# A decoder layer on one core: in the first feed-forward product, three of eight pairs of weight tiles by seven products, and part of the weight sums added by accumulating transfers

## The chip, the cores and the metric

The kernel runs on one core of a Trainium2 chip. The metric is the device time of one execution in microseconds; the lower the better.

## The reference

One layer of a decoder: a token mixer (an mLSTM group and a dilated attention group), cross-attention into 256 memory tokens, and a SwiGLU feed-forward part, each followed by a residual and a layer norm. All is float32; there are 256 tokens of width 2048. The change lies in the products with `w1` and `w3` (2048 x 5632 each):

```python
def swiglu_ffn(x, w1, w3, w2):
    return (jax.nn.silu(x @ w1) * (x @ w3)) @ w2
...
    y = swiglu_ffn(x, w1[l], w3[l], w2[l])
    x = layer_norm(DEEPNORM_ALPHA * x + y, ln_g[l, 2], ln_b[l, 2])
```

## The kernel before

**Three products for one.** TensorE takes fp32r operands. Each float32 operand is split into a rounded part (`h`, a copy by ScalarE, ACT) and the rest (`l`, a subtraction by VectorE, DVE), both in `split` (L110, L111), and a product is h·h + h·l + l·h: three matmuls of 128x512 for each block.

**The groups.** The first feed-forward product is cut by columns. `f0` is made by `gemm_tokens`; then ten groups `f2`, `f4`, ... `f20` follow, each with 1024 columns (two blocks of 256 of `w1` and of `w3`) by all 2048 rows of weight. The rows are taken as eight *pairs* of tiles, numbered 0 to 7, of two tiles of 128 rows each. Between `f10` and `f12` stand `w2a0` and `w2a1`, the first half of the second feed-forward product; `w2b0` and `w2b1` are the second half. After each group `hidden` takes silu of one half times the other, transposes the result on TensorE (tiles `f8p0`, `f8p1` for group f8), and puts the split transpose into `hT`.

**Plain pairs and pairs by seven products.** A plain pair is 2 tiles x 4 output blocks x 3 = 24 matmuls. For a pair written as a tuple in `plan`, `gemm_seven` uses the scheme with seven products for the eight of a 2x2 by 2x2 block product: 7 x 3 = 21 matmuls. It needs sums of the activations (`mix`, kept for the whole stage as `x2m`) and sums of the weights of the pair. `sums` makes these on DVE in two slots: `t` (two sums, L308, one instruction over 1024 columns) and `s` (two more, L312 and L313, 512 columns each, the second from the first). Of the four tiles that are then split, one is 512 wide and three are 1024 wide. The banks P5, P7 and Q6 belong to the sums; P1, P2, P3, Q4 and E are also or only those of the plain products.

**Buffers.** The weights of a pair (1 MB) come into one of three buffers `w` (`RAW` = 3) by two transfers on SP's queue (SyncE); split tiles go into five `wh`/`wl` buffers (`SPLIT` = 5). Everything else lies in `NSLOT` slots of 128x1024 that `big` takes from the front of a list and `free` puts at its end; `slot` hands out halves of such a slot. A tile that gets a slot waits for the last reader of the tile before it there.

**Order.** A scheduler (in `TileContext`) sets each engine's order at build time from a timeline of its own. On the chip each engine, and each of SP's and GpSimd's (POOL's) queues of transfers, then works strictly in that order, and waits by semaphores.

Of the kernel before, what the change touches and what calls it, by code (L numbers as in the profile page):

```python
# [50 lines left out]
def decoder_layer(ctx: ExitStack, tc: tile.TileContext, A):  # L51
    nc = tc.nc
    V, SC, G, T = nc.vector, nc.scalar, nc.gpsimd, nc.tensor
    CONV = V

    const = ctx.enter_context(tc.tile_pool(name="const", bufs=1))
# [12 lines left out]
    def big(name, dt=F32R):  # L69
        i = free_slots.pop(0)  # L70
        t = up.tile([P, 1024], dt, tag=f"u{i}", name=name)
        held[id(t)] = (i, t)
        return t

    def slot(name):
        if len(free_halves) < 3 and free_slots:
            t = big(name, F32)
            i, _ = held.pop(id(t))
            pair = {"i": i, "free": 2}
            for c in range(2):  # L80
                free_halves.append((t[:, c * 512 : (c + 1) * 512], pair))
        t, pair = free_halves.pop(0)
        pair["free"] -= 1
        held[id(t)] = (pair, t)
        return t

    def free(*tiles):
        for t in tiles:
            where, _ = held.pop(id(t))
            if isinstance(where, int):  # L90
                free_slots.append(where)
                continue
# [27 lines left out]
    class Operand:  # L120
# [79 lines left out]
    def fetch_pair(src, name):  # L200


        def get(b):
            w = wp.tile([P, 2, W], F32, tag="w", name=f"{name}w{b}", bufs=RAW)
            for c in range(2):
                nc.sync.dma_start(
                    out=w[:, :, c * 512 : (c + 1) * 512],
                    in_=src[c][b // 2][:, b % 2].rearrange("p (s c) -> p s c", s=2),
                )
            return w  # L210

        return get

    def plain(get, b, name, kept=()):

# [80 lines left out]
                    op.free(order[n] // 2)  # L296
        return banks

    def sums(get, b, name):

        w = get(b)
        t, t2 = big(f"{name}t{b}", F32), big(f"{name}s{b}", F32)
        q = w.rearrange("p i (c n) -> p (i c) n", c=2)

        V.tensor_tensor(  # L308
            out=t.rearrange("p (c n) -> p c n", c=2), in0=q[:, 0::3], in1=q[:, 1:2].to_broadcast([P, 2, 512]),
            op=ALU.add,  # L310
        )
        V.tensor_tensor(out=t2[:, :512], in0=t[:, :512], in1=q[:, 3], op=ALU.add)  # L312
        V.tensor_tensor(out=t2[:, 512:], in0=t2[:, :512], in1=q[:, 2], op=ALU.add)  # L313
        for to, x, n in (("P1", w[:, 0], 1), (("P2", "P3"), w[:, 1], 2), (("P5", "P7"), t, 2), (("Q6", "Q4"), t2, 2)):
            wh = wp.tile([P, W], F32R, tag="wh", name=f"{name}h{b}")
            wl = wp.tile([P, W], F32R, tag="wl", name=f"{name}l{b}")
            cs = slice(0, 512 * n)
            split(wh[:, cs], wl[:, cs], x[:, cs])
            for i, k in enumerate((to,) if n == 1 else to):
                yield k, wh, wl, slice(i * 512, (i + 1) * 512)  # L320
        free(t, t2)

    def gemm_seven(op, get, nkt, name, plan, early, order=None, kept=range(0), last=False):

        order = order or list(range(nkt))
        of = {i: bank(f"{name}{i}") for i in ("P2", "P3", "Q4", "E", "P1")}  # L330
        of |= {i: sbank(f"{name}{i}") for i in ("P5", "P7", "Q6")}
        banks = [[of["P2"], of["P3"]], [of["Q4"], of["E"]]]
        begun = set()
        final = [b for b in plan if isinstance(b, int)][-1]
        final7 = [b for b in plan if not isinstance(b, int)][-1][0]

        def product(to, lhsT, rhs, end):
            T.matmul(of[to], lhsT, rhs, start=to not in begun, stop=end)  # L338
            begun.add(to)

        def tile_products(m, n, wh, wl, cols=range(2)):
            xh, xl = (op.get(order[n], x, m * P, P) for x in (0, 1))
            for c in cols:
                cs, to = slice(c * 512, (c + 1) * 512), (("P2", "P3"), ("Q4", "E"))[m][c]
                product(to, xh, wh[:, cs], False)
                product(to, xh, wl[:, cs], False)
            for c in cols:
                cs, to = slice(c * 512, (c + 1) * 512), (("P2", "P3"), ("Q4", "E"))[m][c]
                product(to, xl, wh[:, cs], n == 2 * final + 1)

        behind = []
        for step in plan:
            if isinstance(step, int):
                for n, wh, wl in plain(get, step, name, kept):
                    tile_products(0, n, wh, wl)
                    if n in kept:
                        behind.append((n, wh, wl))
                    else:
                        tile_products(1, n, wh, wl)
                b = step  # L360
            else:
                (b,) = step
                j = order[2 * b] // 2
                for to, wh, wl, cs in sums(get, b, name):
                    xh, xl = (op.of_product(to, j, x) for x in (0, 1))
                    product(to, xh, wh[:, cs], False)
                    product(to, xh, wl[:, cs], False)
                    product(to, xl, wh[:, cs], b == final7 and to in ("P1", "P5", "P7", "Q6"))
                if b == final7:
                    early(of)  # L370
            if last and 2 * b not in kept:
                op.free(order[2 * b] // 2)
        for c in range(2):
            for n, wh, wl in behind:
# [38 lines left out]
    def turned(rows, j, name):  # L413
# [15 lines left out]
        out=tri, in_=tri, pattern=[[1, P]], compare_op=ALU.is_ge, fill=NEG, base=0, channel_multiplier=-1  # L429
# [246 lines left out]
    def into_rows(rows, name):  # L676


        def early(of):
            u = slot(f"{name}u")  # L680
            for m in range(2):
                rows.append([slot(f"{name}{m}{c}") for c in range(2)])
            (r11, r12), (r21, r22) = rows
            SC.copy(r11, of["P1"])
            V.tensor_tensor(out=u, in0=r11, in1=of["Q6"], op=ALU.subtract)
            V.tensor_tensor(out=r21, in0=u, in1=of["P7"], op=ALU.add)
            V.tensor_tensor(out=r12, in0=of["P5"], in1=u, op=ALU.subtract)
# [78 lines left out]
    sel_t = slot("sel")  # L766
# [3 lines left out]
    nc.sync.dma_start(out=cw, in_=A["conv"])  # L770
    gb = const.tile([8, 1], F32, tag="gb", name="gb")
    nc.sync.dma_start(out=gb, in_=A["gate_b"])
    gw = const.tile([P, KT, 8], F32, tag="gw", name="gw")
    nc.sync.dma_start(out=gw, in_=A["w_gate"])

    gw2 = const.tile([P, KT, 40], F32R, tag="gw2", name="gw2")
    gz = slot("gwz")
    V.memset(gz, 0.0)
    V.tensor_copy(gw2[:, :, 8:32], gz.rearrange("p (k c) -> p k c", k=KT)[:, :, :24])
# [6 lines left out]
        attention(2 * j, qk0[j], qk0[2 + j], [va[m][0] for m in range(2)], tb)  # L786
    qk1 = in_features(2) + in_features(3)
    es, least_norm = gates()
    free(sel_t)
    for j in range(2):  # L790
        attention(4 + 2 * j, qk1[j], qk1[2 + j], [va[m][1] for m in range(2)], tb)
    free(*va[0], *va[1])
# [14 lines left out]
    for c in range(2):  # L807
        t = slot(f"mg{c}")
# [34 lines left out]
    order = list(range(8, 16)) + list(range(8))  # L843
# [3 lines left out]
    for g in range(2):  # L847
        get, plan = fetch(A["w_out"][g], f"wo{g}"), [0, 2, (1,), 4, 5, (3,), 6, 7]
# [88 lines left out]
    plan = [0, 2, (1,), 4, (3,), 5, 6, 7]  # L937
# [5 lines left out]
    x2 = Operand("x2")  # L943
# [47 lines left out]
            for m in range(2):  # L991
                add(m, c, banks, scale=1.0)

    for j in (2, 5):
        x2.mix_again(j)
    for g in range(2, n, 2):
        get, rows = fetch_pair(A["w13"][g - 2 : g], f"f{g}"), []
        plan = [0, 1, (2,), 3, 4, (5,), 6, 7]
        banks = gemm_seven(x2, get, KT, f"f{g}", plan, into_rows(rows, f"f{g}r"), last=g == n - 2)
        whole(rows, banks)  # L1000
        hidden(g, rows, lambda b, i: [b[i][:, x * 256 : (x + 1) * 256] for x in range(2)], f"f{g}")
        free(*rows[0], *rows[1])
        if g == half - 2:
            w2_first()
# [115 lines left out]
```

## Time and profile before

| | |
|---|---|
| runs | 1546.26, 1546.54, 1547.52 us; median 1546.54 |
| the profiled execution | 1546.63 us, of which the span of the instructions is 1544.8 us |
| TensorE | 1526.1 us busy, 99% of the span |
| VectorE, ScalarE, GpSimd | 77%, 50%, 2% of the span |
| transfers | 301.35 MB, mean 195 GB/s |

In the profile, PE is TensorE's matmuls, PEld its loads of the stationary operand, DVE VectorE, ACT ScalarE, POOL GpSimd, and SPq the transfers that SP issues. A row of instructions has its start, its duration, the engine, the line of the kernel, and what it writes and reads; in brackets stands the time for which the engine was idle before it, and what ended that. Matmuls overlap, so the duration of one is longer than the distance from one to the next.

### The profile page before, as it was taken

Reading aid. Unit: us, or ns where it says so; the run is one execution under the profiler, and the core shown is the slowest. Engines: PE = TensorE matmul, PEld = TensorE weight load, DVE = VectorE, ACT = ScalarE, POOL = GpSimd, SP = SyncE. Lnnn points to the kernel's source line nnn. Section 1 sums busy time; section 2 is a strip of 40 time slices with the busy share of each in tenths; the row PEclk is TensorE's granted clock in tenths of the full one; section 3 lists DMA queues with packets and bytes.
Section 4 is the critical chain, followed back from the end, with each engine's and each line's share of the span. In section 5 each row is a group of like instructions: output and inputs, shape, how many; then the busy total and the mean of one; then the engine's idle time right before and its main releaser. Section 6 shows DMA issues by size and latency. Waiting matters only on the chain.

```text
span 1544.8 us, 19283 instructions
## 1 busy us (share of the span) xinstructions
PE 1526.1 (99%) x7410; PEld 1277.2 (83%) x7410; DVE 1192.9 (77%) x1584; ACT 775.7 (50%) x1011; POOL 30.9 (2%) x30
## 2 busy tenths in 40 slices
PE   9999999999999999999999999999999999999997
PEld 7888888888888888888887888887788888888885
DVE  7665888787789655557788678887788878888897
ACT  5445555554544544444544554555445455555551
POOL 0000000000000000000014000000000000000000
PEclk9999999999999999999999999999999999999999
DMA  8674445674664546445553565665465656668552
GB/s 302 215 266 162 151 171 207 221 256 144 228 214 168 212 169 215 167 139 193 187 191 136 171 210 191 217 193 192 162 218 192 206 191 193 199 193 268 197 189 108
DMA packets 83354, 301.35 MB, mean 195 GB/s; under 512 B 7181, under 2 KB 9402, under 8 KB 59710
## 3 DMA queue, kind: packets, MB, share of 16 engines
q1 hardware_dynamic: 83262, 300.12, 56.3%
q8 instruction: 58, 0.95, 0.2%
q14 instruction: 34, 0.28, 0.1%
HBM read 297.97 MB, written 4.21 MB: 196 GB/s over the span
## 4 chain that ended last, share of the span: by engine, by line
PE 95%; DVE 3%; DMA 1%; issue 1%; ACT 0%; SPq 0%; DVEq 0%; ACTq 0%
PE w2a1P L338 2%; PE w2a0P L338 2%; PE w2b0P L338 2%; PE w2b1P L338 2%; PE f10P L338 2%; PE f20P L338 2%; PE v1P L338 2%; PE xo0P L338 2%; PE xo1P L338 2%; PE v0P L338 1%; PE f18P L338 1%; PE f8P L338 1%; PE wo0P L338 1%; PE f4P L338 1%; PE f2P L338 1%; PE f6P L338 1%
## 5 line engine op out<-in xcount | busy, mean ns | idle before, releaser
L257 DVE TENSOR_TENSOR xv1l<-xv1w,xv1h 128x1024 fp32r<-128x1024 f32 x16 | 19.6, 1224 | 20.7 <-ACT xv1h L256 20.6
L257 DVE TENSOR_TENSOR xv0l<-xv0w,xv0h 128x1024 fp32r<-128x1024 f32 x16 | 19.6, 1225 | 20.0 <-ACT xv0h L256 20.0
L110 ACT CAST w2a1h<-w2a1w 128x1024 fp32r<-128x1024 f32 (+1 forms) x24 | 22.5, 980 | 23.3 <-PE w2a1E L338 14.5
L110 ACT CAST w2a0h<-w2a0w 128x1024 fp32r<-128x1024 f32 (+1 forms) x24 | 22.8, 980 | 17.8 <-PE w2a0E L338 10.7
L111 DVE TENSOR_TENSOR w2a0l<-w2a0w,w2a0h 128x1024 fp32r<-128x1024 f32 (+1 forms) x24 | 26.5, 1131 | 6.1 <-ACT w2a0h L110 6.1
L111 DVE TENSOR_TENSOR w2a1l<-w2a1w,w2a1h 128x1024 fp32r<-128x1024 f32 (+1 forms) x24 | 26.4, 1131 | 5.6 <-ACT w2a1h L110 5.6
L256 ACT CAST xv1h<-xv1w 128x1024 fp32r<-128x1024 f32 x16 | 16.9, 1055 | 23.8 <-PE xv1b L276 17.2
L256 ACT CAST xv0h<-xv0w 128x1024 fp32r<-128x1024 f32 x16 | 16.9, 1055 | 21.6 <-PE xv0b L276 16.4
L110 ACT CAST w2b0h<-w2b0w 128x1024 fp32r<-128x1024 f32 (+1 forms) x20 | 19.2, 988 | 16.8 <-PE w2b0E L338 10.1
L338 PE MATMUL w2a0P<-w2a0h,hT 128*128 128x512 f32 x80 | 26.2, 391 | 0.2 <-ACT w2a0h L110 0.2
L257 POOL TENSOR_TENSOR f0l<-f0w,f0h 128x512 fp32r<-128x512 f32 x12 | 20.0, 1696 | 314.6 <-ACT f0h L256 314.6
L110 ACT CAST w2b1h<-w2b1w 128x512 fp32r<-128x512 f32 (+1 forms) x28 | 19.8, 758 | 12.5 <-PE w2b0E L338 5.4
L338 PE MATMUL w2a1P<-w2a1h,hT 128*128 128x512 f32 x80 | 25.4, 389 | 0.0
L110 ACT CAST wo1h<-wo1w 128x1024 fp32r<-128x1024 f32 (+1 forms) x16 | 15.6, 1000 | 18.9 <-PE wo1E L338 11.3
L110 ACT CAST f12h<-f12w 128x1024 fp32r<-128x1024 f32 (+1 forms) x16 | 15.6, 1000 | 18.7 <-PE f12E L338 11.3
L273 PE MATMUL f0b<-f0l,x 128*128 128x512 f32 x64 | 24.9, 405 | 0.1
L273 PE MATMUL xv0b<-xv0l,mT 128*128 128x512 f32 x64 | 25.0, 391 | 0.0
L111 DVE TENSOR_TENSOR w2b0l<-w2b0w,w2b0h 128x1024 fp32r<-128x1024 f32 (+1 forms) x20 | 22.2, 1139 | 3.6 <-ACT w2b0h L110 3.6
L272 PE MATMUL xv1b<-xv1h,mT 128*128 128x512 f32 x64 | 24.9, 392 | 0.0
L272 PE MATMUL xv0b<-xv0h,mT 128*128 128x512 f32 x64 | 24.9, 389 | 0.0
L273 PE MATMUL xv1b<-xv1l,mT 128*128 128x512 f32 x64 | 24.9, 389 | 0.0
L272 PE MATMUL f0b<-f0h,x 128*128 128x512 f32 x64 | 24.7, 407 | 0.0
(1641 smaller groups left out, 5488.4 us busy)
## 6 DMA issues: line engine op xcount, KB each, us to landing
w2a0w<-in_w SPq DMA_DIRECT2D x12, 1024.0 KB, 4.9
w2a1w<-in_w SPq DMA_DIRECT2D x12, 1024.0 KB, 5.2
w2b0w<-in_w SPq DMA_DIRECT2D x10, 1024.0 KB, 4.9
w2b1w<-in_w SPq DMA_DIRECT2D x10, 1024.0 KB, 5.0
v0w<-in_w_v SPq DMA_DIRECT2D x8, 1024.0 KB, 5.2
v1w<-in_w_v SPq DMA_DIRECT2D x8, 1024.0 KB, 4.9
v2w<-in_w_v SPq DMA_DIRECT2D x8, 1024.0 KB, 4.9
wo0w<-in_w_out SPq DMA_DIRECT2D x8, 1024.0 KB, 6.0
```

The source lines that it names most:

```text
L110: SC.copy(hi, src)
L111: V.tensor_tensor(out=lo, in0=src, in1=as_f32(hi), op=ALU.subtract)
L256: SC.copy(wh[:, cs], w[:, i, cs])
L257: eng.tensor_tensor(out=wl[:, cs], in0=w[:, i, cs], in1=as_f32(wh[:, cs]), op=ALU.subtract)
L272: T.matmul(banks[m][c], xh, wh[:, cs], start=n == 0, stop=False)
L273: T.matmul(banks[m][c], xh, wl[:, cs], start=False, stop=False)
L338: T.matmul(of[to], lhsT, rhs, start=to not in begun, stop=end)
```

## The change

The plan of each of the ten groups goes from two to three pairs by seven products, and these stand as the second, fourth and sixth of the eight steps; before they were the third and the sixth. Correspondingly three activation sums `x2m` are made instead of two. Of the weight sums, `t` is no longer added by DVE: two transfers on SP's queue write one block of weights each into the halves of `t` (0.26 MB each), and a transfer on POOL's queue then reads a third block, once for each half, and adds it to what lies there (`accum_op`, 0.52 MB written). `s` is still made by DVE. There are 35 slots in place of 34; to pay for one, the gate weights `gw` and `gw2` move from places of their own into slots that are freed again.

```diff
-NSLOT, RAW, SPLIT = 34, 3, 5
+NSLOT, RAW, SPLIT = 35, 3, 5
...
-        return get
+        def part(b, s, c):
+            return src[c][b // 2][:, b % 2].rearrange("p (s c) -> p s c", s=2)[:, s : s + 1]
+
+        def get_sums(b, t):
+            t = t.rearrange("p (c n) -> p c n", c=2)
+            nc.sync.dma_start(out=t[:, 0:1], in_=part(b, 0, 0))
+            nc.sync.dma_start(out=t[:, 1:2], in_=part(b, 1, 1))
+            G.dma_start(out=t, in_=part(b, 0, 1).to_broadcast([P, 2, 512]), accum_op=ALU.add)
+
+        return get, get_sums
...
-    def sums(get, b, name):
+    def sums(get, b, name, get_sums=None):
+        t = big(f"{name}t{b}", F32)
+        if get_sums:
+            get_sums(b, t)
         w = get(b)
-        t, t2 = big(f"{name}t{b}", F32), big(f"{name}s{b}", F32)
+        t2 = big(f"{name}s{b}", F32)
         q = w.rearrange("p i (c n) -> p (i c) n", c=2)
-        V.tensor_tensor(
-            out=t.rearrange("p (c n) -> p c n", c=2), in0=q[:, 0::3], in1=q[:, 1:2].to_broadcast([P, 2, 512]),
-            op=ALU.add,
-        )
+        if not get_sums:
+            V.tensor_tensor(
+                out=t.rearrange("p (c n) -> p c n", c=2), in0=q[:, 0::3],
+                in1=q[:, 1:2].to_broadcast([P, 2, 512]), op=ALU.add,
+            )
...
-    gw = const.tile([P, KT, 8], F32, tag="gw", name="gw")
+    gw_t, gw2_t = slot("gw"), big("gw2")
+    gw = gw_t[:, :128].rearrange("p (k c) -> p k c", k=KT)
...
-    gw2 = const.tile([P, KT, 40], F32R, tag="gw2", name="gw2")
+    gw2 = gw2_t[:, :640].rearrange("p (k c) -> p k c", k=KT)
...
-    free(sel_t)
+    free(sel_t, gw_t, gw2_t)
...
-    for j in (2, 5):
+    for j in (1, 4, 6):
         x2.mix_again(j)
     for g in range(2, n, 2):
-        get, rows = fetch_pair(A["w13"][g - 2 : g], f"f{g}"), []
-        plan = [0, 1, (2,), 3, 4, (5,), 6, 7]
-        banks = gemm_seven(x2, get, KT, f"f{g}", plan, into_rows(rows, f"f{g}r"), last=g == n - 2)
+        rows, plan = [], [0, (1,), 2, (4,), 3, (6,), 5, 7]
+        get, get_sums = fetch_pair(A["w13"][g - 2 : g], f"f{g}")
+        banks = gemm_seven(
+            x2, get, KT, f"f{g}", plan, into_rows(rows, f"f{g}r"), last=g == n - 2, get_sums=get_sums
+        )
```

In most groups the scheduler lets the transfers of a `t` run a whole group ahead; those of `f4t4` stand ahead of the first weights of f2. In f10 it does not. The next rows are VectorE's in f10 before, around the sum `f10s2` of its first pair by seven products: `hT8`, `hT9` and `hTm8` are the results of f8 that are put away, `f10l2` are splits of pair 2, `f10l6` is one of the plain pair 3.

```order
L111 TENSOR_TENSOR hT9_8833<-f8p1_8828,hT9_8833 128x2x256 [waits Activation_49]
L144 TENSOR_TENSOR f8ru_8720<-f8r11_8723,f8ru_8720 128x128 [waits DVE_49]
L111 TENSOR_TENSOR f10l2_8940<-f10t2_8917,f10h2_8939 128x1024 [waits Activation_49]
L111 TENSOR_TENSOR hT8_8814<-f8r11_8723,hT8_8814 128x2x256 [waits Activation_49]
L111 TENSOR_TENSOR hTm8_8821<-f8ru_8720,hTm8_8821 128x512 [waits Activation_49]
L312 TENSOR_TENSOR f10s2_8918<-f10t2_8917,f10w2_8914 128x512 [waits DVE_49]
L313 TENSOR_TENSOR f10s2_8918<-f10s2_8918,f10w2_8914 128x512 [waits DVE_49]
L111 TENSOR_TENSOR f10l2_8950<-f10s2_8918,f10h2_8949 128x1024 [waits Activation_49]
L111 TENSOR_TENSOR f10l6_8963<-f10w3_8959,f10h6_8962 128x1024 [waits DMAHW5_49,DMAHW4_49,Activation_49]
```

The same place now, where the first pair by seven products is pair 1 and the second is pair 4; `f10l4_8998` and `f10l5_9014` are the splits of the plain pair 2 that stands between them.

```order
L111 TENSOR_TENSOR hT9_8901<-f8p1_8896,hT9_8901 128x2x256 [waits Activation_49]
L144 TENSOR_TENSOR f8ru_8788<-f8r11_8791,f8ru_8788 128x128 [waits DVE_49]
L111 TENSOR_TENSOR hT8_8882<-f8r11_8791,hT8_8882 128x2x256 [waits Activation_49]
L326 TENSOR_TENSOR f10s1_8954<-f10t1_8947,f10w1_8951 128x512 [waits DVE_49]
L111 TENSOR_TENSOR hTm8_8889<-f8ru_8788,hTm8_8889 128x512 [waits Activation_49]
L327 TENSOR_TENSOR f10s1_8954<-f10s1_8954,f10w1_8951 128x512 [waits DVE_49]
L111 TENSOR_TENSOR f10l1_8985<-f10s1_8954,f10h1_8984 128x1024 [waits Activation_49]
L326 TENSOR_TENSOR f10s4_9036<-f10t4_9029,f10w4_9033 128x512 [waits DMAHW7_49,DMAHW2_49,DMASW6_49]
L111 TENSOR_TENSOR f10l4_8998<-f10w2_8994,f10h4_8997 128x1024 [waits DMAHW5_49,DMAHW4_49,Activation_49]
L111 TENSOR_TENSOR f10l5_9014<-f10w2_8994,f10h5_9013 128x1024 [waits Activation_49]
```

The sum `s` still stands behind `hT8`; the row that adds `f10t4`, which waits for an accumulating transfer (DMASW), now stands ahead of the plain splits. Following `big` and `free` through the code, `f10s1` gets the slot in which `hidden` of f8 had kept the copy that `hT8` is made from, as `f10s2` did before; and `f10t4` gets the slot of `f8h10` and `f8h11`, whose last readers are the transposes into `f8p1`.

TensorE at this place before: the last transposes of f8 and what follows. After them 13 plain matmuls of pairs 0 and 1 follow (three are shown) before the first of pair 2.

```order
L967 MATMUL f8p0_8807<-ident_75,f8r11_8723 128x128 [waits DVE_49]
L967 MATMUL f8p0_8807<-ident_75,f8r01_8722 128x128
L967 MATMUL f8p0_8807<-ident_75,f8r11_8723 128x128
L967 MATMUL f8p1_8828<-ident_75,f8t0_8812 128x128 [waits DVE_49]
L967 MATMUL f8p1_8828<-ident_75,f8t0_8812 128x128 x2
L338 MATMUL f10E_8839<-f10h1_8863,x20_6997 128x512
L338 MATMUL f10Q4_8838<-f10h2_8882,x21_7000 128x512
L338 MATMUL f10Q4_8838<-f10l2_8883,x21_7000 128x512
```

TensorE now: the first `Q6` row reads the ScalarE copy `f10h1_8984` of the sum `f10s1`.

```order
L982 MATMUL f8p0_8875<-ident_75,f8r11_8791 128x128 [waits DVE_49]
L982 MATMUL f8p0_8875<-ident_75,f8r01_8790 128x128
L982 MATMUL f8p0_8875<-ident_75,f8r11_8791 128x128
L982 MATMUL f8p1_8896<-ident_75,f8t0_8880 128x128 [waits DVE_49]
L982 MATMUL f8p1_8896<-ident_75,f8t0_8880 128x128 x2
L352 MATMUL f10P7_8910<-f10h1_8974,x2m1_7404 128x512 [waits Activation_49]
L352 MATMUL f10P7_8910<-f10l1_8975,x2m1_7404 128x512
L352 MATMUL f10P7_8910<-f10h1_8974,x2m1_7404 128x512
L352 MATMUL f10Q6_8911<-f10h1_8984,x2m1_7404 128x512 [waits Activation_49]
L352 MATMUL f10Q4_8906<-f10h1_8984,x21_6995 128x512
L352 MATMUL f10P2_8904<-f10h4_8997,x22_7003 128x512 [waits Activation_49]
L352 MATMUL f10P3_8905<-f10h4_8997,x22_7003 128x512
```

Counted in the program's order, 35 matmuls of f10 stood ahead of this batch of transposes and 63 ahead of the first that reads the copy of the sum `s`; now it is 36 and 39. The fiftieth matmul is the last ahead of the first that reads `f10l4_8998`.

SP's queue in f10 now; the weights `f10w3` stand behind the two plain transfers of `f10t4`. On POOL's queue the accumulating transfers stand in the order `f10t1`, `f10t6`, `f10t4`.

```order
L206 DMA f10w4_9033<-in_w13 128x2x512 [waits DMAHW7_49,DMAHW6_49,DVE_49]
L206 DMA f10w4_9033<-in_w13 128x2x512
L218 DMA f10t6_9111<-in_w13 128x512 [waits DMAHW0_49,DVE_49]
L219 DMA f10t6_9111<-in_w13 128x512 [waits DMAHW1_49]
L218 DMA f10t4_9029<-in_w13 128x512 [waits DMASW3_49,DMAHW2_49,DVE_49,PE_49]
L219 DMA f10t4_9029<-in_w13 128x512 [waits DMAHW3_49]
L206 DMA f10w3_9076<-in_w13 128x2x512 [waits DMAHW4_49,DVE_49]
```

Before, nothing but the sixteen transfers of `f10w` and those of the next stage stood on this queue. In the whole program TensorE's order has 30 matmuls fewer; its order also changes here and there in the token mixer, where the slots are handed out differently.

More of the change, by code (lines that the diff above doesn't have):

```diff
@@ L321, in sums, with gemm_seven @@
         free(t, t2)
-    def gemm_seven(op, get, nkt, name, plan, early, order=None, kept=range(0), last=False):
+    def gemm_seven(op, get, nkt, name, plan, early, order=None, kept=range(0), last=False, get_sums=None):
         order = order or list(range(nkt))
@@ L363, in gemm_seven @@
                 j = order[2 * b] // 2
-                for to, wh, wl, cs in sums(get, b, name):
+                for to, wh, wl, cs in sums(get, b, name, get_sums):
                     xh, xl = (op.of_product(to, j, x) for x in (0, 1))
```

## Prediction

> **What bounds the kernel now.** I read the profile's page first: the span, the busy shares, and the shares of the chain that ended last.
>
> ```profile
> span 1544.8 us, 19283 instructions
> PE 1526.1 (99%) x7410; PEld 1277.2 (83%) x7410; DVE 1192.9 (77%) x1584; ACT 775.7 (50%) x1011; POOL 30.9 (2%) x30
> PE 95%; DVE 3%; DMA 1%; issue 1%; ACT 0%; SPq 0%; DVEq 0%; ACTq 0%
> q1 hardware_dynamic: 83262, 300.12, 56.3%
> ```
>
> TensorE sets the time, and a matmul saved counts in full where it does not begin to wait. The transfers took 56% of the sixteen engines' time, all of them on the hardware queue: no accumulating transfer is in this trace. Then I cut the stage: a plain group (f4), f10, and f16, a group in which a fetch came late. The columns are the stretch, its length, the busy time of each engine with its instructions, granted clock, share and rate of transfers.
>
> ```profile
> core 0: us, PE busy (x) PEld busy (x) DVE busy (x) ACT busy (x) POOL busy (x), PEclk, DMA share, GB/s
> 911.66:954.76 43.10, 43.10 (x195) 35.66 (x195) 36.15 (x47) 23.33 (x29) 0.00 (x0) 1.00 0.61 196
> 1040.99:1085.26 44.27, 43.70 (x196) 35.53 (x195) 34.96 (x45) 23.53 (x29) 0.00 (x0) 1.00 0.57 190
> 1298.50:1342.26 43.76, 43.52 (x195) 35.41 (x194) 36.51 (x47) 23.65 (x29) 0.00 (x0) 1.00 0.60 192
> ```
>
> In a plain group TensorE never stops: 43.10 of 43.10 us, clock 1.00. f10 already loses 44.27 − 43.10 = 1.17 us and f16 loses 0.66 us. The chain of waits gives the step of a matmul and, in f10, the transposes and the place where ScalarE takes over the chain.
>
> ```profile
> 911.66 5.44 PE f4P L338 x24
> ...
> 1040.99 5.44 PE f10P L338 x24
> ...
> 1049.18 0.65 PE f8p L967 x6
> ...
> 1056.43 1.05 ACT f10h L110
> 1057.53 0.73 PE f10P L338 x2
> ```
>
> A matmul takes 5.44 / 24 = 0.2267 us and a transpose 0.65 / 6 = 0.108 us. A group has 6 x 24 + 2 x 21 = 186 matmuls and 8 transposes: 42.17 + 0.87 = 43.04 us, which is the 43.10 read.
>
> **What is removed.** Three matmuls in each of ten groups: 30 x 0.2267 = −6.80 us, all on the path if the cover holds; a group then takes 42.4 us.
>
> **What is added on VectorE and ScalarE.** The next rows are f4's groups of instructions, with mean ns of one behind the bar.
>
> ```profile
> L111 DVE TENSOR_TENSOR f4l<-f4w,f4h 128x1024 fp32r<-128x1024 f32 x11 | 13.3, 1220 | 4.4 <-ACT f4h L110 4.4
> L110 ACT CAST f4h<-f4w 128x1024 fp32r<-128x1024 f32 x10 | 10.1, 1054 | 5.8 <-PE f4E L338 5.8
> L313 DVE TENSOR_TENSOR f4s<-f4s,f4w 128x512 f32<-128x512 f32 x2 | 1.4, 684 | 0.0
> L111 DVE TENSOR_TENSOR f4l<-f4w,f4h 128x512 fp32r<-128x512 f32 x2 | 1.4, 684 | 0.0
> L110 ACT CAST f4h<-f4w 128x512 fp32r<-128x512 f32 x2 | 1.2, 612 | 0.7 <-ACT f4h L110 0.7
> L308 DVE TENSOR_TENSOR f4t<-f4w 128x1024 f32<-128x1024 f32 x1 | 1.2, 1217 | 0.0
> ```
>
> A pair that turns from plain to seven has three splits of 1024 and one of 512 in place of two of 1024, and two sums of 512: on VectorE 1.22 + 0.68 + 2 x 0.68 = +3.3 us, on ScalarE 1.05 + 0.61 = +1.7. Two L308 go, −2.4. VectorE is then busy 36.15 + 0.9 = 37.0 of 42.4 us (87%), ScalarE 25. TensorE's matmuls hide both; without that cover it would be at most 0.9 us a group, since VectorE's total stays below TensorE's. The third `x2m` costs a copy, four blocks and a split on VectorE:
>
> ```profile
> L152 DVE TENSOR_TENSOR x2r<-x 128x512 f32<-128x512 f32 x1 | 0.7, 692 | 0.0
> L141 DVE TENSOR_TENSOR x2r<-x2r 128x128 f32<-128x128 f32 x1 | 0.3, 285 | 0.0
> 850.72 6.67 DVE L257 TENSOR_TENSOR f0l<-f0w,f0h 128x1024 fp32r<-128x1024 f32 x5 [4.60 <-ACT f0h L256]
> ```
>
> 0.69 + 4 x 0.28 + 0.69 = 2.5 us, once. During f0 VectorE has an idle gap of 4.60 us; I take 0, and 2.5 if the gap is gone. The slots for `gw`, `gw2` and the moved order in the token mixer: no row prices them; the nearest is f10's own loss of 1.17, so 0 ± 1.
>
> **f10, the largest term.** Slots are scarcest here, because `hT` has grown. The rows are VectorE's, ScalarE's and TensorE's around the sum `f10s2` of before, in order of time.
>
> ```profile
> 1049.55 0.59 ACT L972 COPY f8r<-f8p 128x512 f32<-128x512 f32 x1 [0.49 <-PE f8p L967]
> 1051.64 1.22 DVE L111 TENSOR_TENSOR f10l<-f10t,f10h 128x1024 fp32r<-128x1024 f32 x1
> 1052.78 0.69 DVE L111 TENSOR_TENSOR hT<-f8r,hT 128x512 fp32r<-128x512 f32 x1
> 1053.38 0.68 DVE L111 TENSOR_TENSOR hTm<-f8ru,hTm 128x512 fp32r<-128x512 f32 x1
> 1053.98 0.68 DVE L312 TENSOR_TENSOR f10s<-f10t,f10w 128x512 f32<-128x512 f32 x1
> 1054.70 0.69 DVE L313 TENSOR_TENSOR f10s<-f10s,f10w 128x512 f32<-128x512 f32 x1
> 1055.48 1.05 ACT L110 CAST f10h<-f10s 128x1024 fp32r<-128x1024 f32 x1 [2.88 <-DVE f10s L313]
> 1056.58 0.50 PE L338 MATMUL f10Q<-f10h,x2m 128*128 128x512 f32 x1 [0.36 <-ACT f10h L110]
> ```
>
> `f10s` takes the slot of f8's copy, so its chain is: transposes, copy, `hT8`, first add, second add, ScalarE's copy, TensorE. Count from f10's first matmul (1040.99). Before, the batch of transposes stood behind 35 matmuls (8.19) and 63 matmuls stood ahead of the sum's reader, so the chain was nearly hidden. Now the batch stands behind 36: 36 x 0.2267 + 2 x 0.108 = 8.38. ScalarE's copy starts 0.37 later, 8.75. From copy to first add it was 1053.98 − 1049.55 = 4.43; the split of `f10t` is no longer in between (−1.14, row to row), and `hTm` now stands behind (−0.60): 11.44. Then `hTm` and the second add at 12.64, ScalarE at +0.78, 13.42 to 14.47, TensorE at 14.5. But TensorE arrives after 39 matmuls and 8 transposes, 8.84 + 0.87 = 9.7: it waits 4.8 us, and about 0.5 more for ScalarE's copy of pair 2's first tile, which comes next. So 5.3 in place of 1.17: **+4.1** from the order alone.
>
> The accumulating transfer follows. VectorE's add that needs `f10t4` now stands ahead of the splits of plain pair 2, and TensorE comes to the first matmul that reads these at 14.5 + 0.5 + 11 x 0.2267 = 17.5. `f10t4` gets the slot that the transposes of f8 free at 8.38 + 0.65 = 9.03; SP then issues two transfers of 0.26 MB (0.42 each, below), the second of which lands after 2.7: 12.2. Then the accumulating one takes X, the add and the split 1.9 more: TensorE goes on at 14.1 + X. What X is, no row shows. The nearest:
>
> ```profile
> f4w<-in_w SPq DMA_DIRECT2D x16, 512.0 KB, 5.1
> xv0w<-in_xv SPq DMA_DIRECT2D x8, 1024.0 KB, 4.9
> z<-in_x SPq DMA_DIRECT2D x6, 256.0 KB, 2.7
> L206 SPq DMA_DIRECT2D f16w<-in_w x16: 367/420/472, 1279.4 to 1320.3; - x16
> L720 POOL TENSOR_TENSOR l1r<-l1r,mhalf 128x1 f32<-128x1 f32 x2 | 2.0, 987 | 3.6 <-DVE l1r L719 3.6
> DVE f16t L308 <- DMA f16w<-in_w: 4.5, 2, 4.0
> ```
>
> (KB, and us from issue to landing; SP's issue min/median/max in ns; in the last row total, times, longest of a wait.) From below X is 2.7: then nothing is added. From above it is two landings one after the other and an instruction of POOL, 2 x 5.1 + 1.0 = 11.2: TensorE stops 7.8 more. It reads and writes 0.52 MB besides fetching 0.52, so I take the row of the same traffic, 5.1, and POOL's 1.0: X = 6.1, TensorE goes on at 20.2 and not 17.5, **+2.8**. f10 thus costs 6.9 more than before.
>
> The Trainium skill, page "DMA: Bandwidth & Descriptors", section "Anatomy of one DMA — SWDGE (gpsimd) path", fits a transfer issued by GpSimd as 2.0 us and its bytes at 436 GB/s; no run here shows one. Taking the bytes twice, 2.0 + 2 x 0.524 / 0.436 gives an estimate for X of 4.4 us, a stop of 1.0, and by that a sum 1.8 us lower than mine, no case of its own. The 1024 KB row above, 4.9 us where the fit has 4.4, leans to my value.
>
> SP's queue: behind `f10t4` stand the weights of pair 3, about 10 us late but needed only after pair 4, 90 matmuls in (20.4 us and the stops). POOL has 30 instructions in all and holds nobody else.
>
> **Contention in the other nine groups.** f4's transfers took 0.61 x 43.10 = 26.3 us of the engines, for 196 GB/s x 43.10 = 8.45 MB: 3.1 us per MB. Added are 3 x 0.52 = 1.57 MB of plain transfers, +4.9 us, and as much accumulated at one or two times the price: 36 to 41 of 42.4 us. It fits, more tightly. A late fetch is in the trace: in f16 VectorE waited 4.0 us for it, and TensorE lost 0.66. Between no group and all nine (5.9) I take two more: **+1.3**.
>
> **Sum:** −6.80 + 6.9 + 1.3 = +1.4. The profiled execution took 1546.63 us, 1.83 more than its span and 0.09 above the median of the runs; 1546.6 + 1.4 = **1548.0**.
>
> **The rivals.**
>
> *The gain arrives.* f10's chain is shorter than I add it up and no fetch comes late. For it: the other nine groups had no stop to speak of and VectorE stays at 87%. Against: even X = 2.7 leaves +4.1 in f10, and that follows from the order. From −6.8 to −6.8 + 3.6: 1539.8 to 1543.4.
>
> *Accumulating transfers slow the weights (ends slower).* The plain and accumulating transfers share the sixteen engines with the weights; an add that waits at a pair's start stands ahead of splits that TensorE needs. It decides from where a weight fetch lands over 4 us late, f16's case, in most groups: nine at 0.66 to 2 us are 6 to 18 on −6.8 + 6.9: 1553 to 1565. Above a price of (42.4 − 31.2) / 4.9 = 2.3 times a plain transfer the engines would bound the group; at 4 times it would be 31.2 + 19.6 = 50.8 us, ten times 7.7 more, over 1620. For it: the share goes from 0.6 to 0.85 or more. Against: the rows show no stage near that limit.
>
> *`f10t4` is late alone.* X = 11.2: 1.3 − 6.8 + 4.1 + 7.8 = +6.4, or 1553.
>
> **How the numbers follow.** Forecast 0.50: f10 at +4.1 to +9, up to three late fetches, 0 ± 1 early, own range 1544 to 1550. The gain arrives 0.20; contention 0.24; `f10t4` late 0.06. A measurement of this kernel tells about 0.2%, 3.1 us, from no change: below 1543.4 is faster, above 1549.6 slower. The forecast gives 0.43 of the 0.50 to the same and 0.07 to slower; faster 0.20, same 0.43, slower 0.07 + 0.24 + 0.06 = 0.37. The range 1542 to 1557 leaves out half of the first rival and about a third of the second with its tail.
>
> **What would show it.** Right: nine groups of about 42.4 us in the chain of waits; in f10 a first `Q` matmul that waits some 4 to 5 us for ScalarE's `f10h`, and a second stop where VectorE waits for `f10t`'s accumulating transfer; f10 at 49 to 51 us; a transfer share of 0.8 or more in the groups. Wrong: f10 under 46 us (the gain arrives), VectorE's adds waiting for `w` or `t` in most groups with TensorE idle at their pairs (contention), or changes in the token mixer above 2 us.

## The result and the profile after

The changed kernel takes 1606.53 us (median; 1602.97 to 1608.96), the kernel before 1546.6 in the same comparison: a ratio of 1.0382, 95% interval 1.037 to 1.0395. It is 60 us slower; the range ended at 1557.

The page of the changed kernel, the same lines as before, and the new queue of GpSimd's transfers:

```profile
span 1606.8 us, 19488 instructions
PE 1542.5 (96%) x7380; PEld 1282.9 (80%) x7380; DVE 1207.7 (75%) x1610; ACT 790.7 (49%) x1032; POOL 65.4 (4%) x60
PE 83%; DMA 8%; DVE 6%; issue 1%; ACT 1%; SPq 0%; DVEq 0%; ACTq 0%
q1 hardware_dynamic: 91902, 315.85, 56.6%
q0 software_dynamic: 8160, 15.73, 5.6%
```

TensorE has the 30 matmuls fewer, yet is busy 16.4 us longer, so the matmuls themselves became slower; and it is idle 64.3 us instead of 18.7 (span less busy time). Transfers hold 8% of the chain instead of 1%. From the first matmul of a stage to the first of the next (us):

| stage | before | changed | difference |
|---|---|---|---|
| start to v2 (token mixer) | 247.6 | 260.3 | +12.7 |
| v2 to f0 | 571.8 | 570.7 | −1.1 |
| f0 | 49.0 | 54.2 | +5.2 |
| f2 | 43.1 | 53.4 | +10.3 |
| f4, f6 | 86.2 | 86.7 | +0.5 |
| f8 | 43.1 | 45.8 | +2.7 |
| f10 | 44.3 | 57.9 | +13.6 |
| w2a0, w2a1, f12 | 170.0 | 170.5 | +0.5 |
| f14 | 43.1 | 49.7 | +6.6 |
| f16, f18 | 87.0 | 85.0 | −2.0 |
| f20 | 43.3 | 56.1 | +12.8 |

So the loss lies at a few places; f6, f16 and f18 take 42.4 to 42.8 us, close to the 42.4 forecast. The stretches f2, f6, f8, f10, f14, f18 and f20 of the changed kernel:

```profile
core 0: us, PE busy (x) PEld busy (x) DVE busy (x) ACT busy (x) POOL busy (x), PEclk, DMA share, GB/s
885.40:938.76 53.36, 47.60 (x192) 37.87 (x192) 37.36 (x44) 27.40 (x33) 2.38 (x2) 0.90 0.76 230
982.66:1025.40 42.74, 42.74 (x192) 34.92 (x192) 36.38 (x48) 25.18 (x31) 2.39 (x2) 1.00 0.76 236
1025.40:1071.31 45.91, 43.71 (x193) 34.92 (x192) 37.46 (x49) 25.38 (x32) 2.38 (x2) 1.00 0.78 231
1071.31:1129.22 57.91, 47.18 (x193) 37.59 (x192) 37.36 (x48) 25.52 (x31) 2.38 (x2) 0.88 0.68 205
1299.75:1349.47 49.72, 45.53 (x193) 37.02 (x192) 36.58 (x48) 25.19 (x31) 3.58 (x3) 0.93 0.82 239
1391.96:1434.40 42.44, 42.44 (x193) 34.99 (x192) 35.53 (x46) 24.62 (x31) 2.38 (x2) 1.00 0.79 248
1434.40:1490.61 56.21, 45.88 (x193) 36.82 (x192) 37.36 (x45) 24.45 (x30) 1.20 (x1) 0.91 0.71 228
```

f6 and f18 have 42.7 and 42.4 us of matmuls and no idle time, with the transfers at 0.76 to 0.79. The four bad groups lose in two columns: idle time (f10: 57.91 − 47.18 = 10.7) and, at a granted clock of 0.88 to 0.93, slower matmuls (f10: 47.18 − 42.4 = 4.8). Over f2, f10, f14 and f20 that is 31 us idle and 16.6 us of slower clock.

What TensorE waited for (its timeline; idle time in brackets), in f2 three times, in f10 twice, in f14 and in f20:

```profile
888.70 0.50 PE L352 MATMUL f2P<-f2h,x 128*128 128x512 f32 x1 [1.58 <-ACT f2h L110]
890.67 0.80 PE L352 MATMUL f2P<-f2h,x 128*128 128x512 f32 x1 [1.47 <-ACT f0h L976]
914.87 0.50 PE L352 MATMUL f2Q<-f2l,x2m 128*128 128x512 f32 x1 [2.63 <-DVE f2l L111]
1085.90 0.79 PE L352 MATMUL f10Q<-f10h,x2m 128*128 128x512 f32 x1 [4.18 <-ACT f10h L110]
1097.07 1.22 PE L352 MATMUL f10P<-f10l,x 128*128 128x512 f32 x2 [6.20 <-DVE f10l L111]
1323.55 0.80 PE L352 MATMUL f14P<-f14l,x2m 128*128 128x512 f32 x1 [4.19 <-DVE f14l L111]
1464.01 0.80 PE L352 MATMUL f20P<-f20l,x2m 128*128 128x512 f32 x1 [9.25 <-DVE f20l L111]
```

And the transfers that the chain of waits names behind these stops:

```profile
871.91 15.60 DMA f2w<-in_w
...
902.35 10.54 DMA f2w<-in_w
...
1085.03 10.13 DMA f10t<-in_w
...
1309.94 10.90 DMA f14w<-in_w
...
1451.28 10.77 DMA f20t<-in_w
```

In f2 and f14 it is a fetch of weights that took 10.5 to 15.6 us (a median of 5.1 and 5.2 before), in f10 and f20 an accumulating transfer that took 10 to 11. In f10 the add for pair 4 waits 8.08 us for the transfer, as forecast, with the splits of pair 2 behind it. In f20 the rows of VectorE show the same blocking: the add for pair 6 waits 11.50 us, and the split of pair 4, which TensorE wants next, stands behind it.

```profile
1095.18 0.69 DVE L326 TENSOR_TENSOR f10s<-f10t,f10w 128x512 f32<-128x512 f32 x1 [8.08 <-DMA f10t<-in_w]
1095.79 2.35 DVE L111 TENSOR_TENSOR f10l<-f10w,f10h 128x1024 fp32r<-128x1024 f32 x2
...
1462.13 0.69 DVE L326 TENSOR_TENSOR f20s<-f20t,f20w 128x512 f32<-128x512 f32 x1 [11.50 <-DMA f20t<-in_w]
1462.74 1.22 DVE L111 TENSOR_TENSOR f20l<-f20t,f20h 128x1024 fp32r<-128x1024 f32 x1
```

How the weights of f2 came to take 15 us: the queues and issues in the 22 us from 868 to 890, around the first matmul of f2 at 885.4 (packets, MB, share of sixteen engines; KB, us to landing).

```profile
q1 hardware_dynamic: 2249, 4.30, 57.2%
q0 software_dynamic: 1073, 2.07, 51.4%
f2w<-in_w SPq DMA_DIRECT2D x8, 512.0 KB, 15.5
f2t<-in_w POOLq DMA_DIRECT2D x2, 512.0 KB, 10.5
```

The shares add up to over 100%: by this measure the engines are full. GpSimd's queue holds 51% of them for 2.07 MB, SP's 57% for 4.30.

### The profile page after: what moved, and what is told of

It is laid out like the page before. It is cut to its first block, busy times and chain, and to the rows that moved or that the text cites. A ratio compares the mean times of both kernels' runs of the same rounds, so it can differ in the third digit from the quotient of the medians.

```text
span 1606.8 us, 19488 instructions
## 1 busy us (share of the span) xinstructions
PE 1542.5 (96%) x7380; PEld 1282.9 (80%) x7380; DVE 1207.7 (75%) x1610; ACT 790.7 (49%) x1032; POOL 65.4 (4%) x60
## 3 DMA queue, kind: packets, MB, share of 16 engines
q0 software_dynamic: 8160, 15.73, 5.6%
## 4 chain that ended last, share of the span: by engine, by line
PE 83%; DMA 8%; DVE 6%; issue 1%; ACT 1%; SPq 0%; DVEq 0%; ACTq 0%
PE w2a0P L352 2%; PE w2b0P L352 2%; PE w2b1P L352 2%; DMA f2w<-in_w 2%; PE f16P L352 1%; PE f10P L352 1%; PE xo0P L352 1%; PE wo0P L352 1%; PE v1P L352 1%; PE v0P L352 1%; PE xo1P L352 1%; PE wo1P L352 1%; PE v2P L352 1%; PE f12P L352 1%; DMA w2a1w<-in_w 1%
## 5 line engine op out<-in xcount | busy, mean ns | idle before, releaser
L267 DVE TENSOR_TENSOR xv1l<-xv1w,xv1h 128x1024 fp32r<-128x1024 f32 x16 | 19.6, 1225 | 20.7 <-ACT xv1h L266 20.6
L110 ACT CAST w2a1h<-w2a1w 128x1024 fp32r<-128x1024 f32 (+1 forms) x24 | 22.6, 980 | 22.5 <-PE w2a1E L352 12.9
L110 ACT CAST w2a0h<-w2a0w 128x1024 fp32r<-128x1024 f32 (+1 forms) x24 | 22.8, 981 | 17.8 <-PE w2a0E L352 10.7
L266 ACT CAST xv1h<-xv1w 128x1024 fp32r<-128x1024 f32 x16 | 16.9, 1055 | 23.8 <-PE xv1b L286 17.2
L266 ACT CAST xv0h<-xv0w 128x1024 fp32r<-128x1024 f32 x16 | 16.9, 1053 | 21.6 <-PE xv0b L286 16.4
L111 DVE TENSOR_TENSOR f2l<-f2w,f2h 128x1024 fp32r<-128x1024 f32 (+1 forms) x16 | 17.4, 1121 | 12.5 <-ACT f2h L110 12.5
L110 ACT CAST f20h<-f20w 128x1024 fp32r<-128x1024 f32 (+1 forms) x16 | 14.9, 968 | 22.1 <-PE f20P L352 10.5
L110 ACT CAST wo1h<-wo1w 128x1024 fp32r<-128x1024 f32 (+1 forms) x16 | 15.6, 1000 | 18.9 <-PE wo1E L352 11.3
```

The lines of the kernel that those rows point to most:

```text
L110: SC.copy(hi, src)
L111: V.tensor_tensor(out=lo, in0=src, in1=as_f32(hi), op=ALU.subtract)
L266: SC.copy(wh[:, cs], w[:, i, cs])
L267: eng.tensor_tensor(out=wl[:, cs], in0=w[:, i, cs], in1=as_f32(wh[:, cs]), op=ALU.subtract)
```

## The experiments

All are timed against the kernel before, in the same comparison 1546.7 to 1547.9 us.

**e1, the slots alone.** In the kernel before:

```diff
-NSLOT, RAW, SPLIT = 34, 3, 5
+NSLOT, RAW, SPLIT = 35, 3, 5
...
-    gw = const.tile([P, KT, 8], F32, tag="gw", name="gw")
-    gw2 = const.tile([P, KT, 40], F32R, tag="gw2", name="gw2")
+    gw_t, gw2_t = slot("gw"), big("gw2")
...
```

> The kernel before with 35 slots in place of 34 and the gate weights in slots; plan of two pairs by seven products and sums by VectorE as before. Theory (the 12.7 us lost in the token mixer come from the slots alone): the first matmul of v2 comes at 260 us and not at 247.6, the feed-forward groups take 43.1 us each, and the time is about 1559 us. Rival (the token mixer's loss hangs on the new plan of the feed-forward part, through the scheduler): v2 at 247.6, about 1546.6 us.

1559.55 us, ratio 1.0082 (1.0067 to 1.0097); v2 begins at 261.9. The token mixer's loss comes from the slots. f0 takes 52.7 here too, so most of f0's loss is theirs as well; f10 gains 1.2 us and w2a0 1.7. Two stretches of e1's mixer around its second stop:

```profile
190.00:200.00 10.00, 7.67 (x44) 6.31 (x42) 3.90 (x12) 2.20 (x7) 0.00 (x0) 1.00 0.08 28
200.00:210.00 10.00, 7.77 (x30) 6.48 (x31) 6.86 (x18) 4.63 (x12) 0.00 (x0) 0.66 0.00 0
```

TensorE is idle for 2.3 and 2.2 us of these stretches, has a mean clock of 0.66 in the second, and almost nothing is transferred; before, it was busy in every one of these 20 us.

**e2, all sums by VectorE.** In the changed kernel:

```diff
-            x2, get, KT, f"f{g}", plan, into_rows(rows, f"f{g}r"), last=g == n - 2, get_sums=get_sums
+            x2, get, KT, f"f{g}", plan, into_rows(rows, f"f{g}r"), last=g == n - 2
```

> The changed kernel with all sums added by VectorE: three pairs by seven products, 35 slots, no transfer for the sums. Theory A (what costs in the feed-forward part is the accumulating transfers): f2, f14 and f20 take 42.4 to 43 us, f10 keeps a first stop of 4 to 5 us for the sum s and what the clock loses after it (47 to 50 us); the token mixer keeps its 12.7; in all 1546.6 + 12.7 - 6.8 + 4 to 8 = 1556 to 1561 us. Rival B (the scarce slots and the order of three pairs by seven products cost it, whoever adds): f2, f14, f20 keep 7 to 13 us each, about 1590 us or more.

1564.79 us, ratio 1.011 (1.0094 to 1.0127), 3.8 above the top of what was expected: the changed kernel loses 41.7 us to something that goes with the transfers. f2, f4, f6, f8, f16, f18 and f20 take 42.4 to 42.5, f14 43.7. f10 takes 51.4, 9.0 over 42.4, without any such transfer: the stop for the sum `s`, and a clock that drops. Its stop, then the whole of f10 and stretches of 1 to 4 us around the stop:

```profile
1071.63 0.79 PE L352 MATMUL f10Q<-f10h,x2m 128*128 128x512 f32 x1 [5.19 <-ACT f10h L110]
```

```profile
1055.92:1107.30 51.38, 45.84 (x193) 36.87 (x192) 39.66 (x50) 25.63 (x31) 0.00 (x0) 0.93 0.52 176
1068.00:1069.00 1.00, 0.00 (x0) 0.00 (x0) 0.93 (x3) 0.45 (x1) 0.00 (x0) 1.00 0.00 0
1070.00:1071.00 1.00, 0.00 (x0) 0.00 (x0) 1.00 (x2) 0.47 (x1) 0.00 (x0) 0.88 0.00 0
1072.00:1073.00 1.00, 1.00 (x3) 0.55 (x3) 1.00 (x2) 1.00 (x2) 0.00 (x0) 0.50 0.97 305
1076.00:1078.00 2.00, 2.00 (x7) 1.53 (x7) 1.93 (x2) 1.01 (x1) 0.00 (x0) 0.60 0.72 240
1078.00:1082.00 4.00, 4.00 (x19) 3.29 (x18) 1.69 (x3) 1.21 (x2) 0.00 (x0) 1.00 1.02 309
```

The stop is 5.19 us; the clock falls to 0.50 within it and stays there until about 1077.6 (a mean of 0.60 from 1076 to 1078), 6 us after TensorE resumed. Matmuls of 42.4 us took 45.84: 3.4 us lost besides the 5.5 idle.

**e3, the third transfer plain.**

```diff
-            G.dma_start(out=t, in_=part(b, 0, 1).to_broadcast([P, 2, 512]), accum_op=ALU.add)
+            G.dma_start(out=t, in_=part(b, 0, 1).to_broadcast([P, 2, 512]))
```

> The changed kernel with GpSimd's transfer as a plain one: it overwrites t with the third block in place of adding it, so this sum is left out; queues, waits, sizes and order as in the changed kernel. Theory A1 (reading and writing back the destination is the price): the transfer lands in about 5 us instead of 10, rates while it is in flight go from 255 to 350 GB/s or more, f14 and f20 lose their stops, 1575 to 1590 us. Rival A2 (the price lies in GpSimd's queue, in the waits and in the order, whatever the transfer does): it still takes 9 to 10 us, 1600 to 1607 us.

1585.84 us, ratio 1.0252 (1.0224 to 1.028): 20.7 less than with accumulation, a time that theory A1 had. Its landing of about 5 us did not come: f20 still takes 54.5 us, since a plain transfer from GpSimd also lands in 8.4 us there, after SP's two; and f10 takes 54.1. Half the cost of the transfers is thus not the adding.

**e4, two pairs by seven products, with accumulating transfers.**

```diff
-    for j in (1, 4, 6):
+    for j in (2, 5):
...
-        rows, plan = [], [0, (1,), 2, (4,), 3, (6,), 5, 7]
+        rows, plan = [], [0, 1, (2,), 3, 4, (5,), 6, 7]
```

> The changed kernel with the plan of before (two pairs by seven products, steps three and six), the sums t still by accumulating transfers, 35 slots. Theory A: twenty accumulating transfers in place of thirty still come beside the weights; f2 and the scarce places f10 and f20 stop for several us each: 1546.6 + 12.7 + 10 to 30 = 1570 to 1590 us. Rival B (three pairs by seven products are what exhausts slots and cover): the groups take 43.1 us, about 1559 us.

1568.06 us, ratio 1.0137 (1.0122 to 1.0152), 8.5 above e1, a little under what was expected; f2 takes 47.7, f4 45.1, f10 46.3; f20, expected to stop, takes 43.2. Twenty such transfers beside the weights of two pairs cost a fifth of what thirty cost beside three.

**e5, the same transfers, and nobody waits.** In the changed kernel:

```diff
         if get_sums:
-            get_sums(b, t)
+            d = big(f"{name}d{b}", F32)
+            get_sums(b, d)
...
-        if not get_sums:
+        if True:
             V.tensor_tensor(
...
         free(t, t2)
+        if get_sums:
+            free(d)
```

> The changed kernel with the same thirty pairs of plain transfers and thirty accumulating transfers, written into a slot of its own that nothing reads; the sums that are used are added by VectorE (as in e2). SP's and GpSimd's queues carry what they carry in the changed kernel, but no add waits for them. Theory A (the price is that the adds, in VectorE's strict order, wait for two transfers in series): f14, f20 at 42 to 43.5 us, f10 at 50 to 52, about 1563 to 1570 us, near e2's 1564.8. Rival C (the transfers themselves are the price: they slow the weights and stand ahead of them on SP's queue): f2, f14 and f20 again 3 to 12 us long, 1585 to 1607 us.

1603.02 us, ratio 1.0373 (1.0354 to 1.0392). Theory A falls as the whole account: with no add waiting the time is nearly as long. But the loss lies in other places (f4 45.4, f6 45.5, f12 50.4 us), and e5 also holds one slot more than the changed kernel; e9 below takes that apart.

**e6, accumulating transfers in six groups.**

```diff
-last=g == n - 2, get_sums=get_sums
+last=g == n - 2, get_sums=get_sums if g in (4, 6, 8, 12, 16, 18) else None
```

> The changed kernel with accumulating transfers in f4, f6, f8, f12, f16 and f18 alone; in f2, f10, f14 and f20, where it stopped, VectorE adds. Theory A (the loss belongs to places where a slot comes free late and an add waits, not to the transfers in flight everywhere): 1564 to 1569 us, e2's 1564.8 within a few us, the six groups 42.4 to 43.5 us. Rival C (contention in every group): the six groups lose 1 to 5 us each, 1572 to 1590 us.

1578.61 us, ratio 1.0205 (1.019 to 1.022), 13.8 above e2. The time is rival C's, but the loss is not in all six groups: f8 takes 46.6 us, the other five 41.5 to 43.6. f20 now takes 42.5 and f10 50.0, so what these two lost beyond e2 belongs to their own transfers. But f2 takes 51.3 and f14 47.5, with their sums by VectorE: there the transfers of f4 and f16, a group ahead, delay the weights.

**e9, e10, e12, e13: the spare slot of e5 with nothing, with SP's two transfers, and with a plain third.** In e5's `get_sums`:

```diff
 e9
-            nc.sync.dma_start(out=t[:, 0:1], in_=part(b, 0, 0))
-            nc.sync.dma_start(out=t[:, 1:2], in_=part(b, 1, 1))
-            G.dma_start(out=t, in_=part(b, 0, 1).to_broadcast([P, 2, 512]), accum_op=ALU.add)
+            G.memset(t[:, :, :8], 0.0)
 e10
-            G.dma_start(out=t, in_=part(b, 0, 1).to_broadcast([P, 2, 512]), accum_op=ALU.add)
 e12
-            G.dma_start(out=t, in_=part(b, 0, 1).to_broadcast([P, 2, 512]), accum_op=ALU.add)
+            G.dma_start(out=t, in_=part(b, 0, 1).to_broadcast([P, 2, 512]))
 e13
-            G.dma_start(out=t, in_=part(b, 0, 1).to_broadcast([P, 2, 512]), accum_op=ALU.add)
+            nc.sync.dma_start(out=t, in_=part(b, 0, 1).to_broadcast([P, 2, 512]))
```

> e5 with no transfers for the spare slot: GpSimd clears 16 columns of it, so that the slot is taken and given back at the same places of the program. Theory C (the transfers themselves make e5's 1603): back near e2, 1562 to 1570 us. Rival D (one slot more being held, and waited for, made e5's loss): 1590 to 1603 us.

> e5 with the two plain transfers on SP's queue alone (0.52 MB per sum), without the accumulating one. If any added traffic in the bursts delays the weights, about half of e5's loss, 1580 to 1590 us; if the accumulating one is what delays them, within 5 us of the run with the slot alone; if the place on SP's queue ahead of the weights is it, all of e5's loss, 1600 us.

> e5 with GpSimd's transfer as a plain one that overwrites the spare slot: same queues, same 0.52 MB fetched, nothing read back and added, nobody waits. If reading and writing back the destination is what delays the weights: near e10's 1567.8, at most 1575 us, against e5's 1603. If a third transfer of 0.52 MB from a second queue is enough, whatever it does: 1590 to 1603 us.

> e12 with the third transfer (plain, overwriting the spare slot) on SP's queue and not on GpSimd's. If it is the second queue, served side by side with the weights, that delays them: near e10's 1567.8, at most 1573 us, and the weights land in about 5 us again. If it is the 0.52 MB more per sum that the bursts can't carry, whatever the queue: near e12's 1586, 1580 to 1590 us.

e9 takes 1568.28 us (ratio 1.0135, 1.0119 to 1.015), e10 1567.84 (1.013, 1.0116 to 1.0144), e12 1586.14 (1.0253, 1.0236 to 1.0271), e13 1587.69 (1.027, 1.0245 to 1.0296), e5 1603.02. e12 lies between its two expectations, the others within one of theirs. So the slot costs 3.5 us over e2 (it also moves stops about: f10 is 3.5 us shorter, f18 and f20 together 5.8 longer), SP's two plain transfers nothing, a plain third from GpSimd 18.3, and reading back and adding 16.9 more.

The weights show the same. Of the fetches whose landing the traces give, the slowest of these groups took 7.5 us in the kernel before, 7.0 in e2, 7.7 in e9 and 7.9 in e10, but 11.9 in e12, 12.1 in e5, 10.4 in e13 and 15.6 in the changed kernel. The weights of f12, and the queue that differs, in e10, e12 and e5:

```profile
q1 hardware_dynamic: 91902, 315.85, 58.1%
f12w<-in_w SPq DMA_DIRECT2D x16, 512.0 KB, 5.4
```

```profile
q0 software_dynamic: 4320, 15.73, 3.9%
f12w<-in_w SPq DMA_DIRECT2D x16, 512.0 KB, 9.8
```

```profile
q0 software_dynamic: 8160, 15.73, 5.7%
f12w<-in_w SPq DMA_DIRECT2D x16, 512.0 KB, 10.1
```

The same 15.73 MB hold the sixteen engines for 0.039 x 1582.6 = 62 us when plain and 0.057 x 1599.3 = 91 us when accumulated: 3.9 and 5.8 us per MB, against 2.9 for SP's transfers in the kernel before (0.563 x 1544.8 / 300.12). The adding makes it 1.5 times as long.

What e5 shows has a limit. Its loss over e9 lies in f2 (6.8 us), f4 and f6 (6.1), f12 and f14 (12.9); f10 has 2.7 of it, f18 and f20 together 0.9. The changed kernel's loss over e2 lies in f2 (11.0), f14 (6.0), f10 (6.5) and f20 (13.7). So transfers that nobody waits for are enough for 35 us in one program; that in the changed kernel the waiting adds cost nothing does not follow. In f10 and f20 the rows above show them waiting 8.08 and 11.50 us. What the wait alone costs there no run isolates, because the spare slot of e5 and e9 moves the stops of just these groups.

In e13 everything is on SP's queue and it is no faster than e12, so a second queue is not what delays. It does not settle that bytes alone do: the third transfer waits there for the first two, with weights behind it.

```profile
SPq L220 <- DMA f4d<-in_w: 18.4, 4, 7.5
f12w<-in_w SPq DMA_DIRECT2D x16, 512.0 KB, 8.0
```

**e7, e8, e11: towards a kernel that keeps the matmuls saved.** e2, with `gw`'s half slot freed at once (e7); e8 and e11 add a plan of their own for f10:

```diff
+    free(gw_t)
...
-    free(sel_t, gw_t, gw2_t)
+    free(sel_t, gw2_t)
...
 e8
-        rows, plan = [], [0, (1,), 2, (4,), 3, (6,), 5, 7]
+        rows, plan = [], [0, 2, (1,), 3, (4,), 5, (6,), 7] if g == 10 else [0, (1,), 2, (4,), 3, (6,), 5, 7]
 e11
-        rows, plan = [], [0, (1,), 2, (4,), 3, (6,), 5, 7]
+        rows, plan = [], [0, 2, (1,), 3, 5, (4,), 6, 7] if g == 10 else [0, (1,), 2, (4,), 3, (6,), 5, 7]
```

> e2 (three pairs by seven products, all sums by VectorE) with the half slot of gw freed as soon as gw2 is made, so that the token mixer has 34 slots beside gw2 as before. If the count of slots makes the mixer's loss: the first matmul of v2 at about 248 us instead of 261.5, and 1564.8 - 12.7 = 1550 to 1553 us. If it is the turn in which slots are handed out: still 8 to 13 us there, 1560 to 1566 us.

> e7 with another plan in f10 alone: [0, 2, (1,), 3, (4,), 5, (6,), 7], so that two plain pairs stand ahead of the first pair by seven products. If f10's loss comes from the short distance between the transposes of f8 and the reader of the sum s, f10 falls from 51.4 to 42.4 to 43.5 us, 8 us less than e7, 1541 to 1545 us, below the kernel before. If scarce slots delay f10 in any plan, it loses 3 us or more against 42.4 still.

> e8 with two pairs by seven products in f10 and not three: [0, 2, (1,), 3, 5, (4,), 6, 7]; all sums by VectorE, gw's half slot freed at once. f10 gives back 0.68 us; if the stage behind it (w2a0, 71.5 us in e8 against 65.3 before) lost its 6 us because the third pair held slots late, it falls to 63.6 to 65.3 and the time is 1541 to 1544 us, below the kernel before; if w2a0 lost them to something else, 1549 to 1550 us.

e7: 1552.15 us, ratio 1.003 (1.0018 to 1.0042), v2 at 249.6 instead of 261.5. With half a slot given back early 12 of the mixer's 14 us are gone, as the count of slots has it (the turn in which they are handed out changes with it). e8: 1549.09, ratio 1.0011 (1.0001 to 1.002), and not the 1541 to 1545 expected. f10 falls from 51.2 to 44.6 and w2a0 rises from 65.3 to 71.5; but eight of f10's matmuls, 8 x 0.2267 = 1.8 us, now stand behind the first of w2a0. By equal work f10 takes 46.4, still 4.0 over 42.4, as the rival has it, and the two stages together take 116.1 instead of 116.5. The longest stop of f10 went from 5.20 to 1.54 us, and w2a0 has one of 1.60: the loss was for the most part moved. e11: 1545.04, ratio 0.9985 (0.9977 to 0.9994), 2.3 us under the kernel before, a difference of 0.15%; f10 44.3, w2a0 65.3, the groups ahead of f10 42.4. It misses the 1541 to 1544 expected, since f0 takes 54.2 instead of 49.0. Why the kernels with 35 slots lose 3 to 6 us in f0 was not settled.

## Why the prediction was wrong, point by point

Of the 61.8 us that the table adds up to, 16.8 lie in the token mixer and f0, where 0 was forecast, 13.6 in f10 (6.9 − 0.7 = 6.2 forecast), 12.8 in f20 (no loss forecast) and 16.9 in f2 and f14 (1.3 for late fetches in all nine groups).

**What was removed** came out as worked: groups without a stop take 42.4 us. VectorE's load was near it (37.0 forecast, 36.38 in f6), and the transfers' mean share in undisturbed groups even lower than forecast (0.85 or more; 0.76 and 0.79 in f6 and f18).

**"The slots for `gw`, `gw2` and the moved order in the token mixer ... 0 ± 1"** failed: +12.7 in the mixer, and most of 5.2 in f0 (e1). The bound came from a row of another stage (f10's own loss). The order showed that TensorE's order moved there; the slots were not counted: 35 less one and a half leaves half a slot fewer than 34, and giving half a slot back took 12 us away (e7).

**f10, the order.** The first stop was forecast as 4.8 + 0.5 us; it is 4.5 with the transfers and 5.5 in e2. The mechanism stands. What was left out is the clock, put at nothing without a reason: 3.4 us in e2, 4.8 in the changed kernel's f10.

**f10, X = 6.1** failed: the transfer took 10.13 us and began 1.5 later than worked out, so TensorE went on at 25.8 and not 20.2. The second stop is 6.2 us, not 2.8 (20.2 − 17.5 makes 2.7). The fit taken from the Trainium skill ("DMA: Bandwidth & Descriptors", section "Anatomy of one DMA — SWDGE (gpsimd) path") gave 4.4, further off still: it has no term for other traffic. The median landings of ten groups' transfers lie between 8.1 and 10.8.

**Contention, +1.3** failed as well. Over e2 the changed kernel loses 17.0 us in f2 and f14, where the trace names late weights; in e5, with nobody waiting for the sums, the transfers cost 35 us over e9. The step compared sums over a group, 36 to 41 us of transfers in 42.4, and found room. By the page's shares an accumulated byte held the engines 1.5 times as long as the same byte plain, within the one to two times assumed; what failed is the mean over a group. Fetches and sums come in bursts, when a buffer or a slot comes free; in the 22 us around the start of f2 the engines were full, though that group's mean was 0.76. And the price of a late fetch was read from f16, 0.66 us for a wait of 4.0 on VectorE; f14 lost 6.6 to a fetch that took 10.9. The rival of contention named this mechanism, but with every group a little late, up to 1565 us, or past 1620 with the engines as the bound of every group; it is a few places, with stops of 1.5 to 9 us and the clock after them.

**f20, a term that is not in the sum.** f20 takes 13.7 us over 42.4, all of it gone in e6, and the rows show its own add waiting. The search for an add that waits ahead of splits was made in f10 alone.

## What to carry to other kernels

A mean share of the transfers says nothing of a burst: ask which fetches are in flight in the ten microseconds around each release of a buffer, and price a new transfer by what it delays there, even if nobody waits for it. Where operations are moved to another queue, look in every stage, not in the tightest alone, for the instruction that waits for them and for what stands behind it on its engine. Buffers taken for small tensors early in a program count like any other: half a slot cost 12 us here, hundreds of microseconds ahead of the stage that was changed.

## What the runs showed of the hardware

TensorE's clock falls to one half within e2's stop of 5.19 us and stays there for 6.0 us of work after it, so that the stop costs 3.4 us more than its idle time. It need not be so long a stop: in f2 of the changed kernel the half comes with the stops of 1.58 and 1.47 us (rows above; a mean clock of 0.53 from 889.0 to 890.7), and again behind the one of 2.63. The half rate lasted 3.4 to 6.0 us of work behind these stops and those of f10, f14 and f20; three stretches of the changed kernel, behind f2's second stop, f10's second and f14's:

```profile
890.70:895.90 5.20, 5.20 (x14) 4.08 (x14) 2.95 (x7) 1.53 (x4) 0.00 (x0) 0.50 0.71 252
1097.10:1100.60 3.50, 3.50 (x8) 2.78 (x9) 3.50 (x5) 0.00 (x0) 0.00 (x0) 0.50 0.34 101
1323.50:1329.40 5.90, 5.86 (x14) 4.65 (x15) 5.90 (x10) 2.38 (x3) 1.20 (x1) 0.50 0.27 94
```

Over the changed kernel, 30 matmuls fewer (−6.8) and 16.4 us more of busy time make 23 us of slower matmuls. Of the stops in f8 the longest was this, and that group's clock is 1.00 above:

```profile
1034.44 0.33 PE L982 MATMUL f6p<-ident,f6t 128*128 128x128 f32 x1 [1.26 <-DVE f6t L977]
```

The Trainium skill, "TensorE: Matmul & The Clock Gate", section "Part 1: The HAM clock gate (the "warmup" mystery)", has the half rate, and the return to full after at least one window of about 3.4 us of sustained work; the half agrees, and so do the 3.4 to 6.0 us measured here.

An accumulating transfer of 0.52 MB holds the sixteen engines for 5.8 us per MB (e5), the same transfer without the adding for 3.9 (e12). Taken one by one, none of the changed kernel's thirty landed within 6 us of its issue; 6.3 was the fastest and 11.9 the slowest.
